# Rotary embedding on half-partition tiles, with two matmul rows in one pair of PSUM banks

## The chip, the cores and the metric

The kernel runs on one core of a Trainium2 chip, the other cores idle. The metric is the time of one execution on the device, in microseconds (us). The span that a profile shows, from the first to the last instruction, is 1.8 to 2.1 us shorter. PE is the matmul engine, DVE the vector engine, ACT the scalar engine, POOL is GpSimd, and SP here only issues transfers. Tiles lie in SBUF; PSUM is the banked memory into which PE writes its sums, and a bank holds 512 fp32 columns in this kernel.

## The reference

The input is 16 batches of 512 rows of 1024 floats. Each row has 16 heads of 64, each head two halves of 32.

```python
x1, x2 = x[..., :half_dim], x[..., half_dim:]          # x: (16, 512, 16, 64)
rotated = np.concatenate([x1 * cos - x2 * sin,
                          x1 * sin + x2 * cos], axis=-1)   # cos, sin: (512, 32)
```

Reading and writing x once is 67 MB. A row costs two products and one sum per element: a cos product, a sin product with the halves of a head swapped, and their sum.

## The kernel before

A tile is two batches: 128 partitions of 8 rows, each a contiguous run of 32 KB. There are 8 tiles, and 5 of them fit in SBUF. In a tile, POOL does the sin products of 7 rows (b1, b2 for pairs of rows, b3 for row 3). DVE does the cos products into PSUM, row 0's sin product and the sums of the three pairs. Rows 0 and 3 are summed by PE, which adds the other product in PSUM with an identity matmul, and ACT copies them out. Row 0 has two banks of its own (`own_ps`), row 3 one bank (`pe_ps`), used twice, half a row at a time.

```python
cos_product(own_ps, rows(0, ROW_OWN), ROW_OWN)
for t in range(NT):
    first, second, third = PAIRS
    b1 = sin_rows(t, first[0], 2)                       # POOL
    p1 = pair_product(t, first[0])                      # DVE, 4 banks (pd)
    r0 = rows(t, ROW_OWN)
    own_product(r0)                                     # DVE
    for ps, r in zip(parts(own_ps), parts(r0)):
        pe_add(ps, swapped(r))                          # PE
    nc.scalar.copy(out=r0, in_=own_ps)                  # ACT
    b3 = sin_rows(t, ROW_PE, 1)
    b2 = sin_rows(t, second[0], 2)
    pair_sum(*p1, b1)
    h0, h1 = zip(parts(rows(t, ROW_PE)), parts(b3))
    pe_half(ROW_PE, *h0)        # DVE product, PE add, ACT copy, in pe_ps
    p2 = pair_product(t, second[0])
    b1 = sin_rows(t, third[0], 2)
    pair_sum(*p2, b2)
    pe_half(ROW_PE, *h1)
    p1 = pair_product(t, third[0])
    if t + 1 < NT:
        cos_product(own_ps, rows(t + 1, ROW_OWN), ROW_OWN)
    pair_sum(*p1, b1)
    stores(t)
# ... loads, tables and helpers cut
```

All loads and stores are issued from SP, in one queue, and in the trace the tiles' transfers land in the order of issue. The sin table comes over ACT's queue.

## Time and profile before

| | before |
|---|---|
| time, median of 6 runs | 162.42 us (162.31 to 162.79) |
| span of the profile | 160.4 us |
| bytes moved | 67.25 MB, 419 GB/s over the span |
| DMA engines' share of the span | 97.9% |
| DVE, POOL busy | 85%, 79% |
| tile of DVE, start to start | 16.97 us (17.02 in the mean of six; one of them waited for a load) |
| first half of the last store issued | 145.90 us |

A line of the timeline is: start, duration, engine, source line, operation, output <- inputs, shapes, count, and in brackets the idle time of the engine just before it with what ended it. The prediction shows the lines of before.

### The profile page before, as it was taken

What the parts mean: (1) busy time and instruction counts of PE and PEld (TensorE: products, weight loads), DVE (VectorE), ACT (ScalarE), POOL (GpSimd) and SP (SyncE); (2) the same over time, 40 slices, a digit from 0 to 9 for tenths busy, and PEclk for the clock granted to TensorE, in tenths of its full rate; (3) what the DMA queues carried; (4) which work ended last, traced back from release to release, by engine and by line L of the source; (5) the groups of instructions that cost most, each with busy time, mean ns of one, the idle gap of its engine ahead of it and who ended that gap; (6) DMA issues with size and microseconds to landing.
All of it is one profiled execution on the core that took longest, in us unless ns stands there. A gap on an engine that the chain in (4) does not pass through costs nothing.

```text
span 160.4 us, 431 instructions
## 1 busy us (share of the span) xinstructions
PE 56.4 (35%) x71; PEld 18.8 (12%) x71; DVE 136.4 (85%) x85; ACT 18.1 (11%) x25; POOL 127.0 (79%) x38
## 2 busy tenths in 40 slices
PE   3043905073505550283209140835055502822000
PEld 0022201030102110121003000301021101210000
DVE  1079879999999999999999999999999999998000
ACT  0003301003100301030101210031003010301000
POOL 1059999999999999988998799982999999960000
PEclk9999985559555855576556855595558555775555
DMA  5999999999999999999999999999999999999994
GB/s 181 408 414 469 392 515 400 392 482 433 392 466 441 400 392 498 417 392 490 419 400 458 449 400 441 458 400 409 482 417 400 482 425 400 466 433 409 417 425 204
DMA packets 2705, 67.25 MB, mean 419 GB/s; under 512 B 272, under 2 KB 400, under 8 KB 400
## 3 DMA queue, kind: packets, MB, share of 16 engines
q1 hardware_dynamic: 2624, 67.18, 97.9%
q10 hardware_dynamic: 80, 0.07, 0.1%
q14 instruction: 1, 0.01, 0.0%
HBM read 33.69 MB, written 33.55 MB: 419 GB/s over the span
## 4 chain that ended last, share of the span: by engine, by line
DVE 43%; DMA 34%; issue 7%; POOL 7%; PE 1%; DVEq 0%; SPq 0%
DVE x L198 21%; DVE pd L150 18%; DMA x<-in_x_dram 18%; DMA out_dram<-x 12%; POOL b L174 7%; DMA b<-in_sin_dram 4%; DVE pe_ps L150 2%; PE pd L122 1%; DVE sns L125 0%; DVE sns L126 0%; DVE own_ps L150 0%; DVE x L159 0%; DVEq L198 0%; SPq L80 0%; DVEq L150 0%
## 5 line engine op out<-in xcount | busy, mean ns | idle before, releaser
L174 POOL TENSOR_TENSOR b<-x,sns 128x2048 f32<-128x2048 f32 (+1 forms) x32 | 126.3, 3981 | 15.3 <-DVE sns L126 8.5
L198 DVE TENSOR_TENSOR x<-pd,b 128x2048 f32<-128x2048 f32 x24 | 54.9, 2287 | 2.3 <-POOL b L174 1.5
L150 DVE TENSOR_TENSOR pd<-x,tab 128x2048 f32<-128x2048 f32 x24 | 55.0, 2291 | 0.2
L185 PE MATMUL own_ps<-x,ident 128*128 128x512 f32 x32 | 29.1, 1064 | 53.5 <-DVE x L159 48.6
L185 PE MATMUL pe_ps<-b,ident 128*128 128x512 f32 x32 | 25.2, 880 | 29.1 <-DVE pe_ps L150 29.1
L185 PEld LDWEIGHTS own_ps<-x,ident 128*128 128x128 f32 x32 | 9.4, 324 | 73.5 <-DVE x L159 59.6
L221 ACT COPY x<-own_ps 128x1024 f32<-128x1024 f32 x8 | 8.1, 1012 | 72.4 <-PE own_ps L185 72.4
L190 ACT COPY x<-pe_ps 128x512 f32<-128x512 f32 x16 | 9.4, 588 | 40.7 <-PE pe_ps L185 40.7
L185 PEld LDWEIGHTS pe_ps<-b,ident 128*128 128x128 f32 x32 | 8.0, 280 | 43.7 <-DVE pe_ps L150 35.9
L150 DVE TENSOR_TENSOR pe_ps<-x,tab 128x512 f32<-128x512 f32 x16 | 11.0, 686 | 0.0
L150 DVE TENSOR_TENSOR own_ps<-x,tab 128x1024 f32<-128x1024 f32 x8 | 9.8, 1224 | 0.2 <-DMA x<-in_x_dram 0.2
L159 DVE TENSOR_TENSOR x<-x,tab 128x1024 f32<-128x1024 f32 x8 | 9.7, 1214 | 0.0
L125 DVE TENSOR_SCALAR sns<-pd 128x256 f32<-128x256 f32 x1 | 0.4, 425 | 7.4 <-PE pd L122 7.4
L122 PE MATMUL pd<-b,spread 64*128 64x256 f32 x2 | 1.2, 696 | 5.1 <-DMA b<-in_sin_dram 5.1
L221 ACT ACT_TABLE_LOAD x1 | 1.3, 1283 | 14.7 <-DVE x L159 14.7
L110 PE MATMUL own_ps<-zero 128*128 128x512 bf16 x2 | 1.0, 622 | 1.2 <-DVE zero L106 1.2
L122 PEld LDWEIGHTS pd<-b,spread 64*128 64x128 f32 x2 | 0.5, 306 | 6.0 <-issue 6.0
L123 PE MATMUL tab<-b,spread 64*128 64x256 f32 x2 | 1.1, 631 | 0.0
L106 DVE MEMSET zero<- 128x256 uint32 x1 | 0.3, 272 | 0.9 <-PEq L252 0.9
L123 PEld LDWEIGHTS tab<-b,spread 64*128 64x128 f32 x2 | 0.7, 333 | 0.2
L110 PE MATMUL pe_ps<-zero 128*128 128x512 bf16 x1 | 0.6, 634 | 0.0
L110 PEld LDWEIGHTS <-zero 128*128 128x128 bf16 x3 | 0.3, 125 | 1.5 <-DVE zero L106 1.2
(9 smaller groups left out, 1.8 us busy)
## 6 DMA issues: line engine op xcount, KB each, us to landing
out_dram<-x SPq DMA_DIRECT2D x5, 4096.0 KB, 25.4
x<-in_x_dram SPq DMA_DIRECT2D x2, 8192.0 KB, 39.1
x<-in_x_dram SPq DMA_DIRECT2D x3, 4096.0 KB, 27.7
out_dram<-x SPq DMA_DIRECT2D x1, 8192.0 KB, 33.0
out_dram<-x SPq DMA_DIRECT2D x2, 2048.0 KB, 10.3
x<-in_x_dram SPq DMA_DIRECT2D x1, 2560.0 KB, 12.0
x<-in_x_dram SPq DMA_DIRECT2D x1, 1536.0 KB, 6.7
b<-in_sin_dram ACTq DMA_DIRECT2D x1, 64.0 KB, 6.9
```

What stands on the lines that cost most here:

```text
L106: nc.vector.memset(zero, 0.0)
L110: nc.tensor.matmul(out=ps, lhsT=zero[:, :P], rhs=zero, start=True, stop=True)
L122: nc.tensor.matmul(out=sin_t, lhsT=spread, rhs=sin_sb, start=True, stop=True)
L123: nc.tensor.matmul(out=cos_t, lhsT=spread, rhs=cos_sb, start=True, stop=True)
L125: nc.vector.tensor_scalar_mul(out=sns[:, :, 0, :], in0=sin_k, scalar1=-1.0)
L150: nc.vector.tensor_tensor(out=o, in0=i, in1=cb, op=ALU.mult)
L159: nc.vector.tensor_tensor(out=heads(r), in0=heads(r), in1=s, op=ALU.mult)
L174: nc.gpsimd.tensor_tensor(out=o, in0=i, in1=sb, op=ALU.mult)
L185: nc.tensor.matmul(out=ps, lhsT=ident, rhs=other, start=False, stop=True, skip_group_check=True)
L190: nc.scalar.copy(out=r, in_=pe_ps)
L198: nc.vector.tensor_tensor(out=r, in0=ps, in1=b, op=ALU.add)
L221: nc.scalar.copy(out=r0, in_=own_ps)
```

## The change

The intent is fewer and longer transfers: with groups of four batches a partition's run in HBM is 64 KB, a tile is half of it, and where two halves lie side by side in the one SBUF buffer they go as one transfer of 8 MB. The tables double (16 rows a partition instead of 8), so the cos table fills a bank and the small table for row 0 needs another. The bank for row 3 has to go; row 3 now uses row 0's two banks.

```diff
-NB = 2
-HOMES = (1, 2, 2)
+NB = 4
+SLOTS = 5
...
-    nc.scalar.dma_start(out=sin_sb, in_=sin_v)
-    load(0, 0, FIRST[0])
+    load(0, 0, FIRST)
+    nc.sync.dma_start(out=sin_sb, in_=sin_v)
     nc.sync.dma_start(out=cos_sb, in_=cos_v)
...
-    load(2)
-    load_two(3)
+    load(2, 0, 2 * KK)
+    load(4)
...
-    pe_ps = pe.tile([P, BANK], FP32)
...
-    nc.vector.tensor_copy(out=sns[:, :, 1, :], in_=sin_k)
+    nc.scalar.copy(out=sns[:, :, 1, :], in_=sin_k)
...
-        if t == 4:
-            store_two(3)
+        if t == 1:
+            store(0, 0, 2 * KK)
...
-            load_two(6)
+            load(6, 0, 2 * KK)
...
         pair_sum(*p1, b1)
-        h0, h1 = zip(parts(rows(t, ROW_PE)), parts(b3))
-        pe_half(ROW_PE, *h0)
         p2 = pair_product(t, second[0])
+        cos_product(own_ps, t, ROW_PE)
+        for ps, b in zip(parts(own_ps), parts(b3)):
+            pe_add(ps, b)
+        nc.scalar.copy(out=rows(t, ROW_PE), in_=own_ps)
         b1 = sin_rows(t, third[0], 2)
         pair_sum(*p2, b2)
-        pe_half(ROW_PE, *h1)
```

Cut: the address arithmetic of the new tiles, the separate buffers for b3, two idle POOL instructions that go, and the parameters that now name the tile's half.

More of the change, by code (lines that the diff above doesn't have):

```diff
@@ L21 @@
 PAIRS = ((1, 2), (4, 5), (6, 7))
-FIRST = (3, 8)
+FIRST = 3
+LAST_OUT = 4
 @with_exitstack
@@ L47 @@
     PB = P // NB
-    KK = seq // PB
-    NT = batch // NB
+    KK = seq // PB // 2
+    NT = 2 * batch // NB
     F = KK * dim
-    x_v = x.rearrange("(t b) (p k) d -> t (b p) (k d)", b=NB, k=KK)
-    out_v = out.rearrange("(t b) (p k) h d -> t (b p) (k h d)", b=NB, k=KK)
-    cos_v = cos.rearrange("(p k) j -> p (k j)", k=KK)
-    sin_v = sin.rearrange("(p k) j -> p (k j)", k=KK)
+    x_v = x.rearrange("(g b) (p k) d -> g (b p) (k d)", b=NB, k=2 * KK)
+    out_v = out.rearrange("(g b) (p k) h d -> g (b p) (k h d)", b=NB, k=2 * KK)
+    cos_v = cos.rearrange("(p k) j -> p (k j)", k=2 * KK)
+    sin_v = sin.rearrange("(p k) j -> p (k j)", k=2 * KK)
     fixed = ctx.enter_context(tc.tile_pool(name="fixed", bufs=1))
@@ L59 @@
     bp = ctx.enter_context(tc.tile_pool(name="bp", bufs=3))
+    b1p = ctx.enter_context(tc.tile_pool(name="b1p", bufs=2))
     pfix = ctx.enter_context(tc.tile_pool(name="pfix", bufs=1, space=bass.MemoryType.PSUM))
@@ L64, with run @@
     ctx.enter_context(tc.manual_schedule())
-    homes = [xp.tile([P, n, F], FP32, name=f"x{n}{i}") for i, n in enumerate(HOMES)]
-    places = [home[:, i] for home, n in zip(homes, HOMES) for i in range(n)]
-    tiles = [places[t % len(places)] for t in range(NT)]
-    first_of = [sum(HOMES[:i]) for i in range(len(HOMES))]
-    def both(t):
-        return homes[first_of.index(t % len(places))]
+    xt = xp.tile([P, SLOTS * F], FP32)
+    def run(t, lo=0, hi=KK):
+        a, b = (t % SLOTS) * F, (t % 2) * F
+        return xt[:, a + lo * dim : a + hi * dim], (t // 2, slice(None), slice(b + lo * dim, b + hi * dim))
     def load(t, lo=0, hi=KK):
-        s = slice(lo * dim, hi * dim)
-        nc.sync.dma_start(out=tiles[t][:, s], in_=x_v[t][:, s])
-    def load_two(t):
-        nc.sync.dma_start(out=both(t), in_=x_v[t : t + 2].rearrange("t p f -> p t f"))
+        place, at = run(t, lo, hi)
+        nc.sync.dma_start(out=place, in_=x_v[at])
     def store(t, lo=0, hi=KK):
-        s = slice(lo * dim, hi * dim)
-        nc.sync.dma_start(out=out_v[t][:, s], in_=tiles[t][:, s])
-    def store_two(t):
-        nc.sync.dma_start(out=out_v[t : t + 2].rearrange("t p f -> p t f"), in_=both(t))
-    tabs = bp.tile([P, 2 * dim], FP32, name="b")
-    sin_sb = tabs[:PB, : KK * half]
-    cos_sb = tabs[:PB, dim : dim + KK * half]
-    nc.scalar.dma_start(out=sin_sb, in_=sin_v)
-    load(0, 0, FIRST[0])
+        place, at = run(t, lo, hi)
+        nc.sync.dma_start(out=out_v[at], in_=place)
+    load(0, 0, FIRST)
+    sin_sb = fixed.tile([PB, BANK], FP32)
+    cos_sb = fixed.tile([PB, BANK], FP32)
+    nc.sync.dma_start(out=sin_sb, in_=sin_v)
     nc.sync.dma_start(out=cos_sb, in_=cos_v)
-    for lo, hi in zip(FIRST, FIRST[1:]):
-        load(0, lo, hi)
+    load(0, FIRST, KK)
     load(1)
-    load(2)
-    load_two(3)
+    load(2, 0, 2 * KK)
+    load(4)
     ident = fixed.tile([P, P], FP32)
     make_identity(nc, ident)
-    for _ in range(2):
-        nc.gpsimd.nop(hint="pause")
     zero = fixed.tile([P, BANK], BF16)
@@ L107 @@
     own_ps = pe.tile([P, dim], FP32)
-    pe_ps = pe.tile([P, BANK], FP32)
-    for ps in (own_ps[:, :BANK], own_ps[:, BANK:], pe_ps):
+    for ps in (own_ps[:, :BANK], own_ps[:, BANK:]):
         nc.tensor.matmul(out=ps, lhsT=zero[:, :P], rhs=zero, start=True, stop=True)
-    sns = fixed.tile([P, KK, 2, half], FP32)
-    tab = pfix.tile([P, BANK], FP32)
-    cos_t = tab[:, : KK * half]
-    sin_t = pd.tile([P, 2 * dim], FP32, name="pd")[:, : KK * half]
+    sns = fixed.tile([P, 2 * KK, 2, half], FP32)
+    cos_t = pfix.tile([P, BANK], FP32)
+    own_t = pfix.tile([P, 2, hd], FP32)
+    sin_t = pd.tile([P, 2 * dim], FP32, name="pd")[:, :BANK]
     spread = fixed.tile([PB, P], FP32)
@@ L123 @@
     nc.tensor.matmul(out=cos_t, lhsT=spread, rhs=cos_sb, start=True, stop=True)
-    sin_k = sin_t.rearrange("p (k j) -> p k j", k=KK)
+    sin_k = sin_t.rearrange("p (k j) -> p k j", j=half)
     nc.vector.tensor_scalar_mul(out=sns[:, :, 0, :], in0=sin_k, scalar1=-1.0)
-    nc.vector.tensor_copy(out=sns[:, :, 1, :], in_=sin_k)
-    own_t = tab[:, KK * half : KK * half + hd]
-    nc.vector.tensor_copy(out=own_t, in_=sns[:, ROW_OWN])
+    nc.scalar.copy(out=sns[:, :, 1, :], in_=sin_k)
     def heads(r):
@@ L137, in rows, with cos_product @@
     def rows(t, k, n=1):
-        return tiles[t][:, k * dim : (k + n) * dim]
-    def cos_product(out, r, k, n=1):
+        return run(t, k, k + n)[0]
+    def cos_product(out, t, k, n=1):
+        r = rows(t, k, n)
+        k += t % 2 * KK
         c = cos_t[:, k * half : (k + n) * half]
@@ L150, in cos_product, with own_product, sin_product @@
         nc.vector.tensor_tensor(out=o, in0=i, in1=cb, op=ALU.mult)
-    def own_product(r):
-        s = bass.AP(
-            tensor=own_t.tensor,
-            offset=own_t.offset + half,
-            ap=[own_t.ap[0], [0, nh], [-half, 2], [1, half]],
-        )
+    def own_product(t, r):
+        o = own_t[:, t % 2]
+        s = bass.AP(tensor=o.tensor, offset=o.offset + half, ap=[o.ap[0], [0, nh], [-half, 2], [1, half]])
         nc.vector.tensor_tensor(out=heads(r), in0=heads(r), in1=s, op=ALU.mult)
-    def sin_product(out, r, k, n):
+    def sin_product(out, t, k, n):
+        r = rows(t, k, n)
+        k += t % 2 * KK
         s = sns[:, k : k + n].rearrange("p k a j -> p (k a j)")
@@ L176, in sin_rows @@
     def sin_rows(t, k, n):
-        b = bp.tile([P, 2 * dim], FP32, name="b")[:, : n * dim]
-        sin_product(b, rows(t, k, n), k, n)
+        b = (bp if n == 2 else b1p).tile([P, n * dim], FP32, name=f"b{n}")
+        sin_product(b, t, k, n)
         return b
@@ L185, in pe_add @@
         nc.tensor.matmul(out=ps, lhsT=ident, rhs=other, start=False, stop=True, skip_group_check=True)
-    def pe_half(k, r, b):
-        cos_product(pe_ps, r, k)
-        pe_add(pe_ps, b)
-        nc.scalar.copy(out=r, in_=pe_ps)
     def pair_product(t, k):
         ps = pd.tile([P, 2 * dim], FP32, name="pd")
-        cos_product(ps, rows(t, k, 2), k, 2)
+        cos_product(ps, t, k, 2)
         return ps, rows(t, k, 2)
@@ L200, in stores @@
     def stores(t):
-        if t == 4:
-            store_two(3)
+        if t == 1:
+            store(0, 0, 2 * KK)
         elif t == NT - 1:
-            store(t, 0, KK // 2)
-            store(t, KK // 2)
-        elif t != 3:
+            store(t, 0, LAST_OUT)
+            store(t, LAST_OUT, KK)
+        elif t > 1:
             store(t)
@@ L209, in stores @@
             load(5)
-            load_two(6)
-    cos_product(own_ps, rows(0, ROW_OWN), ROW_OWN)
+            load(6, 0, 2 * KK)
+    cos_product(own_ps, 0, ROW_OWN)
     for t in range(NT):
@@ L216 @@
         p1 = pair_product(t, first[0])
+        if t == 0:
+            nc.vector.tensor_copy(out=own_t, in_=sns[:, ROW_OWN::KK].rearrange("p k a j -> p k (a j)"))
         r0 = rows(t, ROW_OWN)
-        own_product(r0)
+        own_product(t, r0)
         for ps, r in zip(parts(own_ps), parts(r0)):
@@ L224 @@
         pair_sum(*p1, b1)
-        h0, h1 = zip(parts(rows(t, ROW_PE)), parts(b3))
-        pe_half(ROW_PE, *h0)
         p2 = pair_product(t, second[0])
+        cos_product(own_ps, t, ROW_PE)
+        for ps, b in zip(parts(own_ps), parts(b3)):
+            pe_add(ps, b)
+        nc.scalar.copy(out=rows(t, ROW_PE), in_=own_ps)
         b1 = sin_rows(t, third[0], 2)
         pair_sum(*p2, b2)
-        pe_half(ROW_PE, *h1)
         p1 = pair_product(t, third[0])
         if t + 1 < NT:
-            cos_product(own_ps, rows(t + 1, ROW_OWN), ROW_OWN)
+            cos_product(own_ps, t + 1, ROW_OWN)
         pair_sum(*p1, b1)
```

## The prediction

> **What bounds the kernel now.** I read the page from the top: busy shares, then the forty slices, then the chain that ended last.
>
> ```profile
> PE 56.4 (35%) x71; PEld 18.8 (12%) x71; DVE 136.4 (85%) x85; ACT 18.1 (11%) x25; POOL 127.0 (79%) x38
> ...
> DMA  5999999999999999999999999999999999999994
> ...
> q1 hardware_dynamic: 2624, 67.18, 97.9%
> ...
> DVE 43%; DMA 34%; issue 7%; POOL 7%; PE 1%; DVEq 0%; SPq 0%
> ```
>
> The busiest thing is neither DVE nor POOL but the 16 DMA engines: 9 in every slice but the first and last, 97.9% of the span. The chain names DVE most often only because it is followed through the stores' releasers. The table of windows, cut where DVE ends its last sum, says what lies at each end:
>
> ```profile
> core 0: us, PE busy (x) PEld busy (x) DVE busy (x) ACT busy (x) POOL busy (x), PEclk, DMA share, GB/s
> 0.00:4.00 4.00, 1.46 (x3) 0.28 (x3) 0.49 (x2) 0.00 (x0) 0.70 (x6) 1.00 0.59 181
> 4.00:147.70 143.70, 54.94 (x68) 18.54 (x68) 135.85 (x83) 18.07 (x25) 126.25 (x32) 0.65 1.01 433
> 147.70:160.40 12.70, 0.00 (x0) 0.00 (x0) 0.02 (x1) 0.00 (x0) 0.00 (x0) 0.50 0.80 343
> ```
>
> 433 GB/s for 144 us, then 12.7 us of stores alone. In the trace's packet records a run of 32,768 bytes takes 1213 ns (27.0 GB/s on each engine), one of 16,384 bytes 611 ns. The packets' times over 16 engines add to 157.3 us; the first starts at 2.4 us, the last ends at 159.8. So there is no gap at all: compute is hidden, with little to spare. The last tile's two halves are issued at 145.9 and 147.7 us, and their packets start at 149.2. How little DVE has to spare shows in one tile of the timeline (DVE, then ACT):
>
> ```profile
> 63.52 2.30 DVE L150 TENSOR_TENSOR pd<-x,tab 128x2048 f32<-128x2048 f32 x1
> 65.72 1.21 DVE L159 TENSOR_TENSOR x<-x,tab 128x1024 f32<-128x1024 f32 x1
> 66.85 2.28 DVE L198 TENSOR_TENSOR x<-pd,b 128x2048 f32<-128x2048 f32 x1
> 69.06 0.68 DVE L150 TENSOR_TENSOR pe_ps<-x,tab 128x512 f32<-128x512 f32 x1
> 69.65 2.29 DVE L150 TENSOR_TENSOR pd<-x,tab 128x2048 f32<-128x2048 f32 x1
> ...
> 77.04 1.22 DVE L150 TENSOR_TENSOR own_ps<-x,tab 128x1024 f32<-128x1024 f32 x1
> 78.17 2.28 DVE L198 TENSOR_TENSOR x<-pd,b 128x2048 f32<-128x2048 f32 x1
> 80.49 2.30 DVE L150 TENSOR_TENSOR pd<-x,tab 128x2048 f32<-128x2048 f32 x1
> ```
>
> ```profile
> 70.64 1.01 ACT L221 COPY x<-own_ps 128x1024 f32<-128x1024 f32 x1 [9.92 <-PE own_ps L185]
> 71.55 0.59 ACT L190 COPY x<-pe_ps 128x512 f32<-128x512 f32 x1
> 77.10 0.59 ACT L190 COPY x<-pe_ps 128x512 f32<-128x512 f32 x1 [4.96 <-PE pe_ps L185]
> ```
>
> The reader is to see that DVE runs back to back, 16.97 us a tile, and that PE and ACT work on own_ps from 66.99 to 71.65 us while DVE is busy with other banks. Eight such tiles fit the DMA's 157 us only with the last one finishing about 2 us before its store has to start.
>
> **What the skill says.** The Trainium skill, "DMA: Bandwidth & Descriptors", section "Where 436 GB/s comes from", gives a ceiling of 435.2 GB/s; this trace agrees, with 433 GB/s held and 432 from 16 x 27.0. So the middle can hardly get faster. The same page, "Latency and other measured facts", has copies slowing for row pitches of 2 MiB and more and not at 512 KiB; the new tiles have a pitch of 64 KB, so I expect no loss, but no run here shows it yet. "PSUM — Partial Sum Buffer", section "PSUM bank collisions raise a hardware error", has engines taking turns on a bank; the trace agrees in that each own_ps product, matmul and copy is apart in time. "TensorE: Matmul & The Clock Gate", Part 1, gives 1.2 GHz cold and 2.4 GHz warm, after about 3.4 us of work; here the second and later fp32 matmul records of own_ps start 0.85 us apart at the low clock, and the pair after them takes half of that.
>
> **The change, part by part.** Transfers: the bytes stay 67.2 MB. Three transfers of 8 MB get runs of 64 KB. From 611 ns and 1213 ns, each packet costs about 8.5 ns beyond its bytes; 384 packets fewer on 16 engines are 24 x 8.5 ns = 0.2 us, if the runs stay whole. Only this can shorten the path that bounds now.
>
> Start: the tables come behind the first load on the same queue, on 32 partitions of 2 KB; the sin table landed at 7.64 us and I put it at 7.8. Their two matmuls have 512 columns instead of 256. The old pair took 7.73 to 9.77; at 0.43 us more for each of four records the sin part ends near 9.9 and the cos part near 11.6. The negated sin, 0.43 us for 256 columns, becomes 0.7. The plain copy goes to ACT, behind it (same bank), 0.6 us, perhaps with the 1.28 us table load in front of it, which stood before the first ACT copy. POOL so starts at 11.3 to 12.6 instead of 9.79. Its third product (b2) ended 11.3 us after its start; from there the rest of the first tile is 8.0 us of DVE. The first tile ends near 31.2 instead of 29.55: 1.7 us later, hidden at first, because the load ring is full until about 51.5 us and the first store (two tiles together) is issued near 49.
>
> Steady tile: two half-row products of 0.59 us (start to start) become one of 1.13, saving 0.05. But row 3 now goes through own_ps, so one buffer is used twice a tile, and DVE has to wait for ACT twice. From tile start: own_ps is copied out by 8.13 us (71.65 - 63.52). DVE now arrives at 7.85, starts row 3 at 8.2 and ends at 9.42: wait 0.35. PE then needs four fp32 records, 3.65 us as in the own row, and ACT 1.01: done at 14.2. DVE, after the second sum and third product, arrives at 13.85: wait 0.4. So 16.95 + 0.35 + 0.4 = 17.7 us at the low clock. If PE is warm for the row-3 block, which starts only 2.4 us after the own block ends, it takes 1.8 and the second wait goes: 17.3. I take 17.55, between them.
>
> End: tile 7 starts at 31.2 + 6 x 17.55 = 136.5 us. Its first half waits for the copy of row 3, at about 13.7 into the tile (between cold and warm): issue at 150.2. From issue to first packet took 1.67 us at the start: 151.9. Both halves are 16 packets an engine of 0.611 us: 161.7. The tail from last packet to the end was 0.55: span 162.2. Time exceeds span by 2.07 (162.47 - 160.4): 164.3. Cold throughout (17.75 a tile, 14.2 at the end) gives 166.0, warm throughout 162.3. The middle of these outcomes, a little above because the start may cost more, is 164.6 us, plus 1.3%. What is won on the transfers, 0.2 us, ends inside the new gap of some 2 us before the last store and is worth nothing.
>
> **Rivals.** First, DMA hides it all: the waits are shorter than I think or PE is warm in most tiles, the last store is issued before about 147.7 and the time is 162.2 to 162.5. For it: DMA is full today and bytes are unchanged. Against: only about 2 us of slack, and I count 1.7 us lost at the start alone. Second, the half-partition tiles slow the packets (pitch 64 KB, or 64 KB runs handled worse): 5% on 24 MB of 67 would be 2.8 us of DMA, largely inside the same gap, so 165 to 166. Against: packets sit on the fabric's ceiling with 32 KB runs. Third, the first store: if the first two tiles end after about 50 us instead of 49, the ring runs dry near 51.5; that gap is not added to the end, as DVE sets the end. Fourth, larger runs speed the DMA: at most 0.2 us, 162.3.
>
> **Range and chances.** The three clock cases span 162.3 to 166.0; the start adds 0.5 either way. I take 162.5 to 166.1. Slower by over 2% needs 165.72, nearly the all-cold case: 0.21. Faster by over 2% needs 159.2, less than the packets' 157 plus both ends: 0.02. Within 2%: 0.77.
>
> **What would show it.** Right: in the slices of DMA one of the last ones falls below 9; the copies out of own_ps release DVE some 0.3 to 0.4 us, up to twice a tile; DVE's tile is 17.3 to 17.8 us; POOL starts after 11 us; the last sum ends near 152 to 153 instead of 147.7. Wrong: no wait of DVE on ACT, 128 packets of 64 KB slower than 2.43 us each, or a DMA that is still full to the end with a longer span.

## The result, and the profile after

The changed kernel took 164.45 us (median of 6 runs, 163.85 to 165.43), before 162.42 us. The ratio is 1.0126, with a 95% interval of 1.009 to 1.0163. A ratio here is the mean time of one kernel's runs over that of the other's of the same rounds, so it is not quite the ratio of the medians.

The profile is of the fastest of the six runs, span 162.0 us. Four lines of its page, the counterparts of those that the prediction shows:

```profile
PE 58.0 (36%) x70; PEld 17.7 (11%) x70; DVE 137.6 (85%) x76; ACT 18.1 (11%) x18; POOL 126.9 (78%) x38
...
DMA  6999999799799899889999989988999999996896
...
q1 hardware_dynamic: 2256, 67.24, 97.1%
...
DMA 32%; DVE 19%; issue 13%; POOL 13%; PE 12%; ACT 4%; SPq 0%; ACTq 0%; POOLq 0%; DVEq 0%
```

Busy shares hardly move. Two things do: the DMA row has a 6 in the fourth slice from the end, and PE and ACT have come into the chain that ends last (PE 1% before, 12% now; ACT was absent). The scattered 7s and 8s earlier are no gaps: a 64 KB packet runs 2.4 us and is booked in the slice in which it starts. The table of windows puts that 6 under a lens:

```profile
core 0: us, PE busy (x) PEld busy (x) DVE busy (x) ACT busy (x) POOL busy (x), PEclk, DMA share, GB/s
148.00:149.00 1.00, 0.87 (x2) 0.00 (x0) 0.96 (x2) 0.05 (x1) 0.00 (x0) 0.50 0.24 98
149.00:150.00 1.00, 0.00 (x0) 0.00 (x0) 1.00 (x1) 0.96 (x1) 0.00 (x0) 0.50 0.00 0
150.00:151.00 1.00, 0.00 (x0) 0.00 (x0) 0.90 (x2) 0.00 (x0) 0.00 (x0) 0.50 0.62 262
151.00:152.00 1.00, 0.00 (x0) 0.00 (x0) 1.00 (x1) 0.00 (x0) 0.00 (x0) 0.50 0.61 262
```

From 149 to 150 us no packet starts, while DVE and ACT still work. In the kernel before that microsecond is full:

```profile
149.00:150.00 1.00, 0.00 (x0) 0.00 (x0) 0.00 (x0) 0.00 (x0) 0.00 (x0) 0.50 1.00 426
```

The last store comes too late, as SP's own timeline shows (its first half):

```profile
149.99 0.33 SPq L82 DMA_DIRECT2D out_dram<-xt  x1
```

In the kernel before it is issued four microseconds earlier:

```profile
145.90 0.33 SPq L84 DMA_DIRECT2D out_dram<-x  x1
```

One of the later tiles shows why; these are DVE's lines at its start, at the two places where it writes the shared banks, and at the next tile's start:

```profile
118.51 2.30 DVE L140 TENSOR_TENSOR pd<-xt,cos_t 128x2048 f32<-128x2048 f32 x1
...
126.91 1.23 DVE L140 TENSOR_TENSOR own_ps<-xt,cos_t 128x1024 f32<-128x1024 f32 x1 [0.45 <-ACT xt L207]
...
133.16 1.23 DVE L140 TENSOR_TENSOR own_ps<-xt,cos_t 128x1024 f32<-128x1024 f32 x1 [0.50 <-ACT xt L215]
...
136.62 2.29 DVE L140 TENSOR_TENSOR pd<-xt,cos_t 128x2048 f32<-128x2048 f32 x1
```

The brackets are new: before, no such line waited for ACT. L207 is the copy of row 0, L215 that of row 3. The eight tiles of DVE start at 13.23, 31.09, 48.56, 65.99, 83.29, 100.55, 118.51 and 136.62 us, so the six whole ones after the first take 17.26 to 18.11 us, 17.59 in the mean. PE's matmul blocks (row 0, then row 3) tell the shortest tile from the longest:

```profile
86.81 3.42 PE L174 MATMUL own_ps<-xt,ident 128*128 128x512 f32 x4 [8.10 <-issue]
92.69 3.28 PE L174 MATMUL own_ps<-b,ident 128*128 128x512 f32 x4 [2.46 <-DVE own_ps L140]
```

```profile
122.03 3.75 PE L174 MATMUL own_ps<-xt,ident 128*128 128x512 f32 x4 [8.11 <-issue]
128.28 3.75 PE L174 MATMUL own_ps<-b,ident 128*128 128x512 f32 x4 [2.50 <-DVE own_ps L140]
```

The mean granted clock (the share of its full speed that PE was allowed) was 0.70 in the first of these tiles and 0.50 in the second. A slower PE block is a longer tile now. It is the blocks that count, not a tile's mean clock: four tiles at a mean of 0.60 took 17.30 to 17.96 us, and the one of 17.96, where row 3's block took 3.61 us, alone had the second wait.

The last tile shows what one block is worth. In this run its row 3 block took 2.43 us. The profiled run of experiment 9, whose kernel differs in the cutting of three transfers alone, met a slow PE there:

```profile
146.19 3.75 PE L175 MATMUL own_ps<-b,ident 128*128 128x512 f32 x4 [2.50 <-DVE own_ps L141]
```

```profile
151.06 0.33 SPq L82 DMA_DIRECT2D out_dram<-xt  x1
```

Its last tile starts 0.21 us earlier (136.41), yet its store is issued 1.07 us later, and the run took 165.39 us. This is probably also why the changed kernel's six runs spread over 1.0% while those of before keep within 0.3%. Only one of the six was profiled, so that last step is argued, not shown; the mean clock of a whole run doesn't sort them (163.85 us at 0.661, 165.08 at 0.705, 165.43 at 0.653).

**The ledger**, from the two traces. DVE's first tile ends 1.52 us later (31.09 against 29.57), the six tiles after it add 3.39 (136.62 - 131.71, less 1.52), and within the last tile the store's first half is ready 0.82 us sooner (13.37 us into the tile against 14.19): 4.09 us in all, 145.90 to 149.99. From the issue to the first packet it takes 0.83 us (149.99 to 150.82). Before, the first engine was free for this store at 148.56, so 145.90 + 0.83 left 1.83 us of slack. 4.09 - 1.83 = 2.26 us should be lost; the last packet ends only 1.63 us later (160.81 against 159.18). The rest comes back because the gap lets the engines line up: before, the slowest engine finished 0.66 us behind the middle one (by the small packets, one for each engine, that end a transfer in the trace), after the gap 0.10. The spans differ by 1.62 us. The ledger is of the changed kernel's fastest run; the medians differ by 2.03 us.

### The profile page after: what moved, and what is told of

Read it like the earlier page. It is cut to its first block, busy times and chain, and to the rows that moved or that the text cites. A ratio compares the mean times of both kernels' runs of the same rounds, so it can differ in the third digit from the quotient of the medians.

```text
span 162.0 us, 421 instructions
## 1 busy us (share of the span) xinstructions
PE 58.0 (36%) x70; PEld 17.7 (11%) x70; DVE 137.6 (85%) x76; ACT 18.1 (11%) x18; POOL 126.9 (78%) x38
## 4 chain that ended last, share of the span: by engine, by line
DMA 32%; DVE 19%; issue 13%; POOL 13%; PE 12%; ACT 4%; SPq 0%; ACTq 0%; POOLq 0%; DVEq 0%
DMA xt<-in_x_dram 18%; POOL b L163 13%; PE own_ps L174 10%; DMA out_dram<-xt 10%; DVE xt L182 10%; DVE pd L140 6%; DMA sin_sb<-in_sin_dram 4%; ACT xt L207 3%; DVE xt L146 1%; PE pd L112 1%; ACT xt L215 1%; DVE own_ps L140 1%; DVE sns L115 0%; ACT sns L116 0%; SPq L78 0%
## 5 line engine op out<-in xcount | busy, mean ns | idle before, releaser
L163 POOL TENSOR_TENSOR b<-xt,sns 128x2048 f32<-128x2048 f32 (+1 forms) x32 | 126.2, 3990 | 15.9 <-ACT sns L116 10.5
L140 DVE TENSOR_TENSOR pd<-xt,cos_t 128x2048 f32<-128x2048 f32 x24 | 55.1, 2295 | 0.8
L182 DVE TENSOR_TENSOR xt<-pd,b 128x2048 f32<-128x2048 f32 x24 | 54.8, 2285 | 0.1
L174 PE MATMUL own_ps<-xt,ident 128*128 128x512 f32 x32 | 29.4, 1075 | 63.8 <-issue 33.7
L174 PE MATMUL own_ps<-b,ident 128*128 128x512 f32 x32 | 23.8, 887 | 19.8 <-DVE own_ps L140 19.8
L140 DVE TENSOR_TENSOR own_ps<-xt,cos_t 128x1024 f32<-128x1024 f32 x16 | 19.6, 1228 | 4.7 <-ACT xt L207 2.8
L174 PEld LDWEIGHTS own_ps<-xt,ident 128*128 128x128 f32 x32 | 9.4, 324 | 83.5 <-issue 76.9
L207 ACT COPY xt<-own_ps 128x1024 f32<-128x1024 f32 x8 | 8.1, 1012 | 86.3 <-PE own_ps L174 86.3
L215 ACT COPY xt<-own_ps 128x1024 f32<-128x1024 f32 x8 | 8.1, 1012 | 35.7 <-PE own_ps L174 30.5
L174 PEld LDWEIGHTS own_ps<-b,ident 128*128 128x128 f32 x32 | 7.1, 243 | 37.2 <-issue 25.4
L146 DVE TENSOR_TENSOR xt<-xt,own_t 128x1024 f32<-128x1024 f32 x8 | 9.7, 1215 | 0.0
```

Of the source, the lines that this page charges most:

```text
L140: nc.vector.tensor_tensor(out=o, in0=i, in1=cb, op=ALU.mult)
L146: nc.vector.tensor_tensor(out=heads(r), in0=heads(r), in1=s, op=ALU.mult)
L163: nc.gpsimd.tensor_tensor(out=o, in0=i, in1=sb, op=ALU.mult)
L174: nc.tensor.matmul(out=ps, lhsT=ident, rhs=other, start=False, stop=True, skip_group_check=True)
L182: nc.vector.tensor_tensor(out=r, in0=ps, in1=b, op=ALU.add)
L215: nc.scalar.copy(out=rows(t, ROW_PE), in_=own_ps)
```

## The experiments

Twelve kernels ran, each in five rounds beside the kernel before. Ratios are to the runs of before.

### 1. Copies cut by bank (a miss)

```diff
-        nc.scalar.copy(out=r0, in_=own_ps)
+        for r, ps in zip(parts(r0), parts(own_ps)):
+            nc.scalar.copy(out=r, in_=ps)
```

and the same for row 3.

> The changed kernel with one edit: each copy out of the two shared PSUM banks is two copies, one bank each, so the first bank is free while PE still adds into the second. Theory (shared banks make DVE wait for ACT twice a tile): the last bank of row 0 is free about 7.7 us into the tile and DVE arrives at 7.85, so both waits go; DVE's tile falls from 17.6 to about 17.0 us, the last tile starts near 132.8 us, the DMA is full again to the end and the time is 162.0 to 162.6 us. Rival 1 (the 64 KB runs and the half-partition tiles slow the DMA): DVE's waits go but the time stays near 164.4. Rival 2 (the late start alone costs it): it stays above 163.5.

Measured: 166.33 us, ratio 1.022 (1.0193 to 1.0247). It failed, and the profile says how. One tile, DVE waiting for ACT, and ACT:

```profile
39.02 1.07 ACT L208 COPY xt<-own_ps 128x512 f32<-128x512 f32 x2 [10.80 <-PE own_ps L174]
40.13 1.23 DVE L140 TENSOR_TENSOR own_ps<-xt,cos_t 128x1024 f32<-128x1024 f32 x1 [0.46 <-ACT xt L208]
```

The two copies run back to back, after the last of PE's four matmuls: in the compiled program the first one waits for the whole buffer, not for its bank. So nothing was freed early, and two copies take 1.07 us where one took 1.01. The tile is 17.83 us in the mean, 0.24 more than in the changed kernel; the longer copies are at most 0.12 of that. Three of its six tiles had both waits, two in the changed kernel, but why was not tested. The run doesn't speak on the rivals; the edit didn't do what it was made for.

### 2. The kernel before, with row 3 in the shared banks alone

```diff
-        h0, h1 = zip(parts(rows(t, ROW_PE)), parts(b3))
-        pe_half(ROW_PE, *h0)
         p2 = pair_product(t, second[0])
+        cos_product(own_ps, rows(t, ROW_PE), ROW_PE)
+        for ps, b in zip(parts(own_ps), parts(b3)):
+            pe_add(ps, b)
+        nc.scalar.copy(out=rows(t, ROW_PE), in_=own_ps)
...
-        pe_half(ROW_PE, *h1)
```

> The kernel before with one edit: row 3 is no longer done in halves in its own bank but as a whole in the two banks of row 0, in the order of the changed kernel; transfers, tables and start stay as before. Theory: DVE's tile grows from 16.97 to about 17.5 us, the last tile starts near 134.6 instead of 131.7, its first half is issued near 148.4 and its packets start near 150, 1 us after the DMA has run dry: 163.2 us (162.5 to 164.5 by PE's clock). Rival 1 (layout of the transfers) and rival 2 (start alone): no change, 162.4.

Measured: 163.20 us, ratio 1.0041 (1.0027 to 1.0055). DVE's tile is 17.50 us (tiles start at 29.14 and, six later, at 134.12), the last tile starts at 134.12, its store is issued at 148.81. DVE's two kinds of wait (us in total, times, longest) and SP's line:

```profile
DVE own_ps L150 <- ACT x L221: 2.8, 7, 0.5
...
DVE own_ps L150 <- ACT x L229: 0.3, 1, 0.3
```

```profile
148.81 0.33 SPq L84 DMA_DIRECT2D out_dram<-x  x1
```

So one part of the change, with transfers, tables and start as before, makes the waits and the longer tile. The store is 2.91 us late, of which 1.83 were slack, and of the remaining 1.1 us the levelling of the engines gives some back (the slowest ends 0.22 us behind the middle one instead of 0.66): 0.7 us in the time.

### 3 and 4. One unused sin product ahead of the first tile

The same line in both kernels, the changed one and the one before:

```diff
+    sin_rows(0, 1, 1)
     cos_product(own_ps, ...)
```

> The changed kernel with one unused sin product of one row (about 2.35 us of POOL) put before the first tile. Theory: DVE and its waits set the end, there is no slack, so the delay comes through almost whole: 1.5 to 2.4 us more, 166.0 to 166.8 us. Rival (DMA sets the end): no change, 164.4.

Measured: 167.04 us, ratio 1.028 (1.0261 to 1.0299), so 2.6 us above the changed kernel's 164.45. The last store is issued 3.19 us later than there (149.99), part of it by a slower PE block in the last tile:

```profile
153.18 2.49 SPq L82 DMA_DIRECT2D out_dram<-xt  x2
```

> The kernel before with the same unused sin product of one row before the first tile. Theory: DMA sets the end and the last store is issued 1.6 to 1.7 us before its turn, so of about 2.3 us of delay only about 0.7 comes through: 163.1 us (162.5 to 163.5). Rival (DVE sets the end already): 164.7.

Measured: 162.69 us, ratio 1.0006 (0.9992 to 1.002): no change. The last store's first half was issued at 147.23 instead of 145.90, still 0.55 us before it was needed (147.23 + 0.83 against 148.61):

```profile
147.23 0.33 SPq L84 DMA_DIRECT2D out_dram<-x  x1
```

The pair says it plainly. The same 2.35 us of POOL work is free in the kernel before and paid in full in the changed one. The DMA set the end and DVE sets it now. With experiment 2 it also says why the parts don't add: a late start alone cost nothing, row 3's move alone 0.7 us, and the changed kernel, which has both, pays 2.0, because there is one slack for the two. The expectation for before was too high (0.7 us): DVE's last tile was 2.03 us late, but its store only 1.33, because the copy of row 3 that it waits for met a faster PE (it started 1.33 us later, 146.62 against 145.29).

### 5. The shared banks as two buffers

```diff
-    own_ps = pe.tile([P, dim], FP32)
+    own_ps = [pe.tile([P, BANK], FP32, name=f"own{i}") for i in range(2)]
...
-        cos_product(own_ps, t, ROW_PE)
-        for ps, b in zip(parts(own_ps), parts(b3)):
+        whole_product(t, ROW_PE)          # two products of 512 columns
+        for ps, r, b in zip(own_ps, parts(rows(t, ROW_PE)), parts(b3)):
             pe_add(ps, b)
-        nc.scalar.copy(out=rows(t, ROW_PE), in_=own_ps)
+            nc.scalar.copy(out=r, in_=ps)
```

and the same for row 0.

> The changed kernel with the two shared banks made two separate buffers: every row that goes through them is done in two halves, each with its own product (0.59 us on DVE, start to start, so 0.05 us more a row), its own matmuls and its own copy, so that the copy of the first half waits for its half alone. Theory (the handing back of the shared banks sets DVE's tile): the second half of row 0 is free 7.7 us into the tile, before DVE arrives at 7.85; both waits go, DVE's tile falls from 17.6 to 17.05 us, the last tile starts near 133 us, the last store is issued before its turn near 149 us, and the time is 162.1 to 162.6 us. Rival (64 KB runs and half-partition tiles slow the DMA, or the copies on ACT are too slow however they are cut): 164 us or more.

Measured: 163.05 us, ratio 1.003 (1.0013 to 1.0046). In the table of groups the 32 half products have one wait left, the first one, for the cos table (busy us, mean ns, then idle before and its releaser):

```profile
L149 DVE TENSOR_TENSOR own<-xt,cos_t 128x512 f32<-128x512 f32 x32 | 20.6, 690 | 1.0 <-PE cos_t L113 1.0
```

No wait for ACT is left; the tile is 17.09 us (31.12 to 133.67 in six), the last store is issued at 146.77, before its turn, and the gap is gone. This is 1.4 us of the 2.0. But 163.05 is above the range that I had given, and the interval excludes 1: with the waits gone something of 0.6 us is left.

### 6. The kernel before with shared banks and a busy PE

Experiment 2 plus matmuls of zeros into the bank that it leaves unused, 4 after row 0's block, 16 after row 3's.

```diff
             pe_add(ps, swapped(r))
+        keep_warm(4)
...
             pe_add(ps, b)
+        keep_warm(16)
```

> The kernel before with row 3 in the two banks of row 0 (as in the earlier run that did this alone), and with idle PE time filled with matmuls of zeros into the bank that is now unused: 4 after row 0's matmuls, 16 after row 3's. Results are right. Theory (the wait is the length of PE's two blocks, 3.7 us at the low clock): PE stays at the high clock, its blocks take about 1.9 us, no wait of DVE on ACT is left, DVE's tile falls from 17.50 to 17.0 us and the time from 163.2 to 162.5 us. Rival (the wait is in the copies or in semaphores, not in PE): the tile stays at 17.5 us and the time at 163.2; if the zeros delay the real matmuls, it is longer.

Measured: 164.06 us, ratio 1.0099 (1.008 to 1.0119), slower than experiment 2. The tile did shrink, to 17.36 us (29.18 to 133.31 in six), and row 3's block runs at the high clock:

```profile
73.41 1.95 PE L185 MATMUL own_ps<-b,ident 128*128 128x512 f32 x4 [1.59 <-DVE own_ps L150]
```

The wait behind row 3's block is gone; row 0's block still begins cold, that is at the low clock (3.37 to 3.75 us), and its wait stays in four of the seven tiles after the first. So PE's time is in the wait, as the theory has it, but the end got later for another reason. The program now has 747 instructions, and its page shows an instruction queue that experiment 2 doesn't have:

```profile
q8 instruction: 1, 0.02, 0.0%
```

This is a 16 KB fetch at 94 us. Between the completions at 91 and 112 us the slowest DMA engine falls from 0.87 to 1.69 us behind the middle one, and stays there to the end (1.68). The last store was in time, so the lag goes into the span. But the lag grows in that stretch without a fetch too, from 0.94 to 1.36 us in experiment 2 and from 0.69 to 1.25 in experiment 7. So the fetch can be only a part of it, and no run takes it away: what makes this lag is not shown.

### 7 and 8. Both kernels without arithmetic

```diff
-    (the body of the loop over tiles)
+        for k in range(KK):
+            r = rows(t, k)[:, :1]
+            nc.vector.tensor_scalar_mul(out=r, in0=r, scalar1=1.0)
         stores(t)
```

The result is wrong; loads, stores and their order stay.

> The changed kernel with its arithmetic taken out (wrong on purpose): each row is only touched by a small DVE operation on one column, so loads, stores and their order stay, and nothing but the DMA sets the end. Theory (the new transfers cost nothing): the same as the stripped kernel before of the same call within 0.3 us, near 162 us, 64 KB packets of about 2.42 us. Rival (the layout slows the DMA): 1 us or more longer than the stripped kernel before.

Measured: 163.06 us, ratio 1.0029 (1.0012 to 1.0047).

> The kernel before with its arithmetic taken out in the same way (wrong on purpose). Theory (DMA sets its end): the same time as the whole kernel before, 162.2 to 162.5 us. If it comes out more than 0.5 us shorter, the kernel before was not quite at the DMA's limit.

Measured: 162.41 us, ratio 0.9994 (0.9979 to 1.0009), the same as the whole kernel before: its compute costs nothing.

The new transfers are not free: 0.65 us, and the two buffers of experiment 5 stopped at just this floor. The packets are not slower. A 64 KB run is one packet of 2.419 us in the median, against twice 1.213 for 32 KB; that saves 24 x 7 ns = 0.17 us on each engine, as expected. What differs is how far apart the engines finish: the middle engine ends at 158.74 and 158.78 us in the two, the slowest 1.26 us later in the changed one and 0.83 in the other.

### 9 to 11. Which part of the transfers, and does it matter in the whole kernel

The 64 KB runs cut into two of 32 KB, in the changed kernel and in its stripped form:

```diff
-    load(2, 0, 2 * KK)
+    load(2)
+    load(3)
```

and likewise for the load of tiles 6 and 7 and the store of 0 and 1.

> The changed kernel with its three 8 MB transfers of 64 KB runs cut into two of 32 KB runs each, issued at the same places; nothing else changes. Theory (DVE sets the end, and what the transfers cost or save ends in the gap before the last store): the same as the changed kernel, ratio to the kernel before 1.010 to 1.016, about 164.4 us. Rival (the long runs are what costs the time): 162.5 to 163.5 us.

Measured: 165.24 us, ratio 1.0144 (1.0105 to 1.0182); the changed kernel had 1.009 to 1.0163. No effect of the length of the runs shows there.

> The stripped changed kernel with its 64 KB runs cut to 32 KB (wrong on purpose, as the stripped one is). It was 0.65 us slower than the stripped kernel before, with its slowest DMA engine 1.3 us behind the middle one at the end instead of 0.8. If the long runs set the engines apart: 162.4 to 162.7 us and a lag of 0.8 us or less. If it is the tables on the load's queue at the start, or the pitch: 163.0 us as before.

Measured: 163.47 us, ratio 1.0052 (1.0032 to 1.0071): no better with short runs. The profile here is of its fastest run (162.86 us), with the slowest engine 0.83 us behind, so it doesn't tell what the others did.

The sin table back on ACT's queue, ahead of the first load, with the long runs kept:

```diff
-    load(0, 0, FIRST)
...
-    nc.sync.dma_start(out=sin_sb, in_=sin_v)
+    nc.scalar.dma_start(out=sin_sb, in_=sin_v)
+    load(0, 0, FIRST)
```

> The stripped changed kernel (wrong on purpose) with the sin table again on ACT's queue, ahead of the first load, and the 64 KB runs kept. If the tables at the start set the engines apart: 162.4 to 162.7 us, and the slowest engine less than 0.4 us behind the middle one after the first tile's load instead of 0.63. If it is the long runs or the pitch: 163.0 us.

Measured: 162.32 us, ratio 0.9995 (0.9979 to 1.0012), the same as the kernel before. After the first tile's load the slowest engine is 0.39 us behind the middle one (0.64 with both tables on SP's queue), at the end 0.75 (1.26). So the stripped kernel's 0.65 us go with the sin table's place in the queues; the long runs and the new pitch stayed, and are not their cause. How the place does it is not shown: of the 0.51 us between the two lags at the end only 0.25 are there after the first tile, and the stripped kernel before began with a lag of 0.15 and still ended with 0.83.

### 12. All three mends

The two buffers of experiment 5, runs of 32 KB, the sin table on ACT's queue.

> The changed kernel with all three mends: two separate banks with row halves, 32 KB runs, the sin table on ACT's queue. Theory: DMA sets the end and the engines stay as close as in the kernel before: 162.3 to 162.7 us, the same as the kernel before and not faster, since bytes and packet times are the same. If one of the mends is not one: 163 us.

Measured: 163.07 us, ratio 1.0034 (1.002 to 1.0048). It misses its range and beats neither the kernel before nor experiment 5. Its compute is in time (the last store begins at 148.67 us as in the kernel before) and the slowest engine ends 0.96 us behind the middle one. So in the whole kernel the moved table shows no gain. Since experiment 11 kept the long runs and this one cut them, the short runs may be what costs here (experiment 10 leans that way, 1.0052 against 1.0029 in experiment 7, with intervals that overlap); the pair of the two buffers with long runs and the moved table was not run, and this stays open.

## Why the prediction was right

The time on record is 164.6 us, the measured 164.45. That it is so close is partly luck. The working itself ends at 164.3, and the last 0.3 was a margin for the start, which cost no more than planned. The steps below are held against the profiled run, the fastest of six at 163.85; the others took up to 165.43. Step by step:

- **DMA full before, the middle not to be sped up.** Right: without arithmetic the kernel before takes the same 162.4 us, and the packets' times did not change.
- **Start.** 31.2 us for the end of the first tile, measured 31.09. Two of its pieces were off and small: the table load that I placed perhaps in front of the sin copy ran at 0.73 us, ahead of everything, and POOL started at 11.78.
- **Tile.** 17.55 us, measured 17.59, and the mechanism is that of the text: DVE waits for ACT at both writes of the shared banks. Experiment 2 makes the waits alone, experiment 5 takes them away alone. The all-cold tile was put too low: 17.75, while a tile at clock 0.50 took 18.11. The tile read for it had a row 0 block of 3.61 us, a wholly cold one takes 3.75: row 0's copy ended 8.37 us into that tile, not 8.13. So DVE lost 0.54 and 0.59 us at the two writes (they start 2.74 and 2.79 us after the product before, 2.20 where nothing waits), not 0.35 and 0.4.
- **End.** Issue of the last store at 150.2 us, measured 149.99, with a last tile that met a partly warm PE (13.37 us from its start to the store); cold it takes 14.65, as in experiment 9, not 14.2. Here two terms of the sum were wrong and cancelled: I had set the packet records 0.65 us too late against the instructions. From issue to first packet it is 0.83 us, not 1.67, and from the last packet to the end of the span 1.24, not 0.55.
- **The slack** of about 2 us was measured as 1.83, and experiments 3 and 4 show that it is gone.
- **What the transfers are worth.** The step that failed: "at most 0.2 us" of gain, to vanish in the gap. By themselves, in the stripped kernel, the new transfers lose 0.65 us, and the loss goes with the sin table's place in the queues. In the changed kernel the engines are level after the gap before the last store (a lag of 0.10 us, 1.20 ahead of it), so a lag from before it doesn't reach the end: the outcome was as I wrote though the sign was not, and that is luck too.
- **The signs.** The late slice fell to 6, POOL started at 11.78, the bracketed waits were 0.21 to 0.50 us, and the last sum ended at 153.21, where I had 152 to 153. None of the signs of being wrong came: 64 KB packets took 2.419 us.

The change lies within the 2% to which I gave 0.77, and the interval of its ratio ends at 1.0163. One outcome doesn't test the chances.

## What to carry to other kernels

Where the DMA is full, look for the last store's issue and subtract it from the time at which its engines come free: that slack, here 1.8 us, is all that a longer compute pipeline may cost, and a change that spends it pays for everything after it in full. One buffer for two uses turns three engines' work into a chain in series, however idle each of them looks in the busy shares; buffers that are handed back in halves (two buffers, not two slices of one) keep it apart. Below half a per cent, in a kernel full of DMA, it is the slowest of the 16 engines that counts, so look at how far apart they finish before praising or blaming packet sizes.

## What the Trainium skill lacked or had wrong

- "DMA: Bandwidth & Descriptors" gives no figure for how far apart the 16 engines end one queue's work: here 0.66 to 1.69 us between the middle and the slowest at the end of a span with no gap. Nor has it what the place of a small load in the queues can cost: a 64 KB table, in the stripped kernel, 163.06 us against 162.32 once it was moved (ratios 1.0029 and 0.9995).
- "Runtime: NRT & Kernel Launch", section "Instruction fetch mechanics", calls the cost of an instruction fetch of 16 KB mostly hidden. Experiment 6 has one such fetch in the run, and the slowest engine's lag rose by 0.82 us where experiment 2, without one, has 0.42. Whether the fetch cost anything is not shown.
- "DMA: Bandwidth & Descriptors", section "Why small descriptors are slow (HBM only)", has some 3 cycles of overhead a packet, besides 32 bytes of descriptor metadata. At the 850 MHz that "Advanced Engine Details and Errata", section "Clock Domains", gives for the DMA engines the 3 cycles are an estimate of 3.5 ns; packets of 16, 32 and 64 KB at 611, 1213 and 2419 ns leave 7 to 9 ns (2 x 611 - 1213 and 2 x 1213 - 2419). How much of that is the metadata no run shows.
- "PSUM — Partial Sum Buffer", section "PSUM bank collisions raise a hardware error", has the rule that two engines must be kept off a bank at the same time, and no page adds up what handing a pair of banks round costs: here a product of 1024 columns on DVE 1.23 us, four fp32 matmul records 3.75 at the low clock, a copy on ACT 1.01, so about 6 us from one writing of the banks to the next.
